# A gate's offset added by TensorE in the accumulation instead of by VectorE behind it

## The chip, the cores and the metric

The kernel runs on one core of a Trainium2 chip. The metric is the device time of one execution in microseconds (us). The engines are TensorE (PE, with its weight loads as PEld), VectorE (DVE), ScalarE (ACT), GpSimd (POOL) and SyncE (SP, which here only issues DMAs); PSUM is the memory that TensorE accumulates in, here eight banks of 128 partitions by 512 float32.

## The reference

One layer of an encoder for 2048 tokens of width 1024, in float32: a norm, a mixer, a second norm, and then a sum of three things that a third norm closes. The lines that matter here are these:

```
x = _layernorm(DEEPNORM_ALPHA * x + mix, ln1_g[i], ln1_b[i])
ffn = _hierarchical_moe(x, w_router_group[i], b_router_group[i], w_router_expert[i],
                        b_router_expert[i], w1[i], w3[i], w2[i])
ple = jax.nn.sigmoid(x @ w_ple_gate[i] + b_ple_gate[i]) * (p[i] @ w_ple_proj[i])
x = _layernorm(DEEPNORM_ALPHA * x + ffn + ple, ln2_g[i], ln2_b[i])
```

The experts (`ffn`) run for the two best of 32 experts for each token. The term `ple` is the embedding: a gate of 1024 by 1024 weights, with an offset `b_ple_gate` of 1024 numbers, times a product of 256 by 1024 weights.

## The kernel before

A tile is 128 tokens; there are 16. A float32 product is made of three fp32r matmuls (`mm3`, L221 to L224): each operand is split into a high and a low part, and high by high, high by low and low by high are accumulated in one PSUM bank. The splits are a cast on ScalarE (L356) and a subtraction on VectorE or GpSimd (L357).

The kernel goes through these stages: mixer, second norm and router; the embedding of tiles 10 and 11 and then 12 to 15 (`embed`, L1255), in among the last routing; the experts, as one long stretch of TensorE work; and the end, tiles 0 to 9, one `stage` each with a `last_stage` for tile 9 (from L1865). The end computes the embedding of its tile, adds the rows that the experts left in memory, and applies the third norm to that tile or to one of 10 to 15.

A gate of 512 columns is eight steps of three matmuls into one bank. With sigmoid(g) = (1 + tanh(g/2)) / 2 it then goes on like this:

- VectorE adds the offset, which stands in a buffer `RB[bp]` as 128 equal rows, and writes the sum to a buffer in `ZB`: L1280 in the embedding (12 times), L1862 in the end (19 times with 512 columns, twice with 256). This read frees the bank.
- ScalarE takes tanh in place in `ZB` (L1282, L1863).
- TensorE makes the product with `p`, two steps of three matmuls, in another bank (`embed_product`).
- VectorE multiplies (1 + tanh) by the product (L1286, L1889, L1925) and adds the result to the tile (L1290, L1892, L1926).

The last stage makes its products first and takes its gate in three parts, of 512, 256 and 256 columns; behind each part come multiplication, addition and statistics (L1928), and behind the third the norm in two halves with a write each (L1936).

In the end the inputs of a gate are transposed tiles that an earlier stage put in memory (`x1Td`), loaded by SyncE as a high and a low part into `FB`. The tile's own steps of the third norm are L1825 (adding an expert's row, twice), L1835 and L1837 on VectorE, L1836 (a square) on ScalarE, and L1849 with the write L1850, which ScalarE issues.

The order of the work is set in three ways. Generators are stepped in turn, one `yield` for some matmuls, and buffers are handed out from pools (`take`, `SR`, `SF`, `SP`, `SZ`), oldest first. A scheduler then places the instructions on each engine's queue by its own model of their times. In the end, VectorE's order is fixed as it is written (`pin`). Each engine runs its queue in order and waits on semaphores.

Of the kernel before, what the change touches and what calls it, by code (L numbers as in the profile page):

```python
# [17 lines left out]
D = 1024  # L18
KD = D // 128
# [164 lines left out]
def hybrid_conv_pool_hmoe_encoder(ctx, tc, x, p, ln0_g, ln0_b, w_in, b_in, conv_w, pool_w, pool_scale,  # L184
                                  w_o, ln1_g, ln1_b, w_rg, b_rg, w_re, b_re, w1, w3, w2, w_pg, b_pg,
                                  w_pp, ln2_g, ln2_b, out):
    nc = tc.nc
# [3 lines left out]
    FB, RB = Parts(), Parts()  # L191
# [29 lines left out]
    def mm3(o, ah, al, bh, bl, start, stop):  # L221
        nc.tensor.matmul(o, ah, bh, start=start, stop=False)  # L222
        nc.tensor.matmul(o, ah, bl, start=False, stop=False)  # L223
        nc.tensor.matmul(o, al, bh, start=False, stop=stop)  # L224

    def bcast(ap, n):
        return bass.AP(tensor=ap.tensor, offset=ap.offset, ap=[[0, 128], [1, n]])
# [28 lines left out]
    pidx = consts.tile([128, 1], F32, name="pidx")  # L256
# [70 lines left out]
    def need(name):  # L327

        if name in jobs:
            gen = jobs.pop(name)  # L330
            n = 0
            while next(gen, DONE) is not DONE:
                n += 1
                if n > 40:
                    bg.step()
            bg.forget(gen)
# [450 lines left out]
    v = RB[:, wrr, :KD * 36].rearrange("p (k e) -> p k e", e=36)  # L787
# [386 lines left out]
    def take(slots, m=1, align=1):  # L1174
        n = 0
        while not slots.has(m, align):
            bg.step()
            n += 1
            assert n < 10000, "no slot"
        return slots.get(m, align)  # L1180
# [74 lines left out]
    def lhs_tile(t, k):  # L1255
        return [FB[:, q, k * 128:(k + 1) * 128] for q in xs[t]]

    def embed(ts, lhs, w, done, halves=(0, 1)):

        for h in halves:  # L1260
            cols = slice(h * 512, (h + 1) * 512)
            bs = {}
            for i in range(0, len(ts), 2):
                bs[ts[i]] = take(SP, 2, 2)
                bs[ts[i + 1]] = bs[ts[i]] + 1
            for i in range(4):
                wh, wl = w(5 * h + i)
                for j in range(2):
                    k = 2 * i + j
                    for t in ts:  # L1270
                        mm3(PS[:, bs[t]], *lhs(t, k), FB[:, wh, j * 512:(j + 1) * 512],
                            FB[:, wl, j * 512:(j + 1) * 512], k == 0, k == KD - 1)
                        yield
                SF.free(wh)
                SF.free(wl)
            wh, wl = w(5 * h + 4)
            for t in ts:
                z = take(SZ)
                v = ZB[:, z, :512]
                nc.vector.tensor_add(v, PS[:, bs[t]], RB[:, bp, cols])  # L1280
                SP.free(bs[t])
                nc.scalar.activation(v, v, AF.Tanh, scale=0.5)  # L1282
                need(f"p{t}")
                b = take(SP)
                yield from embed_product(t, PS[:, b], wh, wl)
                nc.vector.scalar_tensor_tensor(v, v, 1.0, PS[:, b], op0=OP.add, op1=OP.mult)  # L1286
                SP.free(b)
                need(f"x{ts[0]}")
                a = RB[:, base[t], cols]
                nc.vector.scalar_tensor_tensor(a, a, ALPHA, v, op0=OP.mult, op1=OP.add)  # L1290
                SZ.free(z)
                if h:
                    release_p(t)
                    done(t)
            SF.free(wh)
            SF.free(wl)
# [37 lines left out]
    for ts in groups:  # L1334
# [9 lines left out]
        c, q = divmod(ts[-1], 4)  # L1344
# [18 lines left out]
    late = ctx.enter_context(tc.tile_pool(name="late", bufs=1))  # L1363
    RB.add(late.tile([128, NY, 1024], F32, name="RY", align_bytes=64), NR, NY)
    SR.add(NR, NY)
    bp = SR.get()
    nc.gpsimd.dma_start(RB[:, bp], bcast(b_pg, D))
    tz = SZ.get()
    prepare(PRE[0])
    w = weight("P", 0)  # L1370
# [90 lines left out]
    for r in ORDER:  # L1461
# [4 lines left out]
        for i in range(HALF[r]):  # L1466
            h = HCUM[r] + i
            f = FCUM[NE] + h // 2
            m = REST[r] if r in WIDE else 64
# [237 lines left out]
    with tc.For_i(0, nov_n, 1) as it:  # L1707
        z, zm = SZ.get(), SZ.get()
# [4 lines left out]
        b = SP.get()  # L1713
        for q in range(2 * NT):
            i, t = divmod(q, NT)
            v = ZB[:, z, (q % 4) * 128:(q % 4) * 128 + 128]
# [75 lines left out]
    def pin(ins):  # L1792

        if pinned:
            tc.add_manual_dep(ins.ins, pinned[-1].ins.name,
                              mybir.DependencyInfo(mybir.DependencyClass.NoSync, mybir.DependencyReason.DATA),
                              reason="in order")
        pinned.append(ins)
# [53 lines left out]

    def gates(t, parts):
        for b, h, lo, hi in parts:
            for k in range(KD):
                wh, wl = (FB[:, q, k % 2 * 512 + lo:k % 2 * 512 + hi] for q in ws[5 * h + k // 2])
                mm3(PS[:, b, :hi - lo], *lhs_tile(t, k), wh, wl, k == 0, k == KD - 1)
                yield

    def gate_end(z, o, cols):  # L1860
        v = ZB[:, z, :cols.stop - cols.start]
        pin(nc.vector.tensor_add(v, o, RB[:, bp, cols]))  # L1862
        nc.scalar.activation(v, v, AF.Tanh, scale=0.5)  # L1863
        return v

    def stage(i, t, ahead, behind):

        if i % 2 == 0 and 6 <= i + 4 < len(END):
            start_fetch(END[i + 4:i + 6])
        need(f"x{t}")  # L1870
        b = take(SP, 2, 2)
        yield from gates(t, [(b, 0, 0, 512), (b + 1, 1, 0, 512)])
        for q in xs.pop(t):
            SF.free(q)
        if i + 2 < len(END) and i % 2 == 0 and i + 2 >= 6:
            need(f"fetch{END[i + 2]}")
        prepare_tile(i + 2)
        zs = [take(SZ), take(SZ)]
        vs = [gate_end(zs[h], PS[:, b + h], slice(h * 512, (h + 1) * 512)) for h in range(2)]
        SP.free(b, 2)  # L1880
        for f in ahead:
            norm_begin(f)
        norm_end()
        need(f"p{t}")
        a = RB[:, base[t]]
        for h in range(2):
            m = take(SP)
            yield from embed_product(t, PS[:, m], *ws[5 * h + 4])
            pin(nc.vector.scalar_tensor_tensor(vs[h], vs[h], 1.0, PS[:, m], op0=OP.add, op1=OP.mult))  # L1889
            SP.free(m)  # L1890
            ah = a[:, h * 512:(h + 1) * 512]
            pin(nc.vector.scalar_tensor_tensor(ah, ah, ALPHA, vs[h], op0=OP.mult, op1=OP.add))  # L1892
            SZ.free(zs[h])
        release_p(t)
        for f in behind:
            norm_begin(f)
            if len(waiting) > 1:
                norm_end()

    def last_stage(t):  # L1900

        need(f"x{t}")
        until(lambda: t in arrived)
        a = RB[:, base[t]]
        need(f"p{t}")
        m = take(SP, 2, 2)
        for h in range(2):
            yield from embed_product(t, PS[:, m + h], *ws[5 * h + 4])
        release_p(t)
        pin(nc.vector.scalar_tensor_tensor(a, a, ALPHA, PS[:, m:m + 2].rearrange("p a c -> p (a c)"),  # L1910
                                           op0=OP.mult, op1=OP.add))
        add_rows(t)
        for i in range(2):
            SR.free(yq.pop((t, i)))
        st = stats[:, 4:6].rearrange("p a b -> p (a b)")
        for lo, hi in ((0, 512), (512, 768), (768, 1024)):
            h, cols, part = lo // 512, slice(lo, hi), slice(lo % 512, (hi - 1) % 512 + 1)
            b = take(SP)
            yield from gates(t, [(b, h, part.start, part.stop)])
            if h == 0:  # L1920
                norm_end()
            z = take(SZ)
            v = gate_end(z, PS[:, b, :hi - lo], cols)
            SP.free(b)
            pin(nc.vector.tensor_mul(v, v, PS[:, m + h, part]))  # L1925
            pin(nc.vector.tensor_add(a[:, cols], a[:, cols], v))  # L1926
            for q in range(lo // 256, hi // 256):
                pin(nc.vector.bn_stats(st[:, 6 * q:6 * q + 6], a[:, q * 256:(q + 1) * 256]))  # L1928
            SZ.free(z)
        nc.vector.bn_aggr(mv[:, 0], st)  # L1930
        nc.vector.tensor_scalar(rstd[:, 0:1], mv[:, 0, 1:2], EPS, None, op0=OP.add)
        nc.gpsimd.tensor_tensor(rstd[:, 0:1], rstd[:, 0:1], mhalf[:, 0:1], op=OP.pow)
        for h, eng in enumerate((nc.sync, nc.scalar)):
            cols = slice(h * 512, (h + 1) * 512)
            ln_apply(a[:, cols], 0, RB[:, g2, cols], RB[:, b2, cols])
            eng.dma_start(outf[t * 128:(t + 1) * 128, cols], a[:, cols])  # L1936
# [45 lines left out]
```

## Time and profile before

| | us |
|---|---|
| median of 3 runs | 1600.15 (1597.69 to 1601.34) |
| profiled execution | 1601.28 |
| its span | 1599.6 |
| PE busy | 1550.9 (97%) |
| DVE busy | 1169.0 (73%) |
| ACT busy | 761.2 (48%) |
| POOL busy | 446.4 (28%) |

The profile is of one execution, and its span is the time from the first instruction to the last event. Busy time of PE counts pipelined matmuls: a row of one lasts longer than the distance to the next start, so distances between starts tell how fast they follow. In a row of a timeline, the bracket at the end gives the idle time of the engine before the instruction and what ended it; x2 stands for two instructions in one row. The granted clock is given as a share of TensorE's full speed.

### The profile page before, as it was taken

Reading aid. Unit: us, or ns where it says so; the run is one execution under the profiler, and the core shown is the slowest. Engines: PE = TensorE matmul, PEld = TensorE weight load, DVE = VectorE, ACT = ScalarE, POOL = GpSimd, SP = SyncE. Lnnn points to the kernel's source line nnn. Section 1 sums busy time; section 2 is a strip of 40 time slices with the busy share of each in tenths; the row PEclk is TensorE's granted clock in tenths of the full one; section 3 lists DMA queues with packets and bytes.
Section 4 is the critical chain, followed back from the end, with each engine's and each line's share of the span. In section 5 each row is a group of like instructions: output and inputs, shape, how many; then the busy total and the mean of one; then the engine's idle time right before and its main releaser. Section 6 shows DMA issues by size and latency. Waiting matters only on the chain.

```text
span 1599.6 us, 22570 instructions
## 1 busy us (share of the span) xinstructions
PE 1550.9 (97%) x7837; PEld 1309.8 (82%) x7837; DVE 1169.0 (73%) x1534; ACT 761.2 (48%) x1005; POOL 446.4 (28%) x628
## 2 busy tenths in 40 slices
PE   8999999999999999989999999999999999999994
PEld 7888878887888887778988998888888888878784
DVE  8968574345666767758879878878888777776987
ACT  6332332113111215037878777777787766662221
POOL 3537763441232225110313111111111010005530
PEclk9999999999999999999999999999999999999997
DMA  7546269986385537459798998999999887998971
GB/s 232 196 144 205 67 199 311 342 300 185 112 271 198 171 116 260 132 205 368 282 364 312 406 373 312 370 350 356 356 353 331 312 328 262 388 328 308 363 232 68
DMA packets 205613, 430.64 MB, mean 269 GB/s; under 512 B 19128, under 2 KB 70888, under 8 KB 205496
## 3 DMA queue, kind: packets, MB, share of 16 engines
q1 hardware_dynamic: 161952, 292.06, 51.1%
q0 software_dynamic: 35024, 125.65, 21.5%
q10 hardware_dynamic: 8520, 11.45, 2.1%
q8 instruction: 63, 1.03, 0.3%
q14 instruction: 54, 0.44, 0.1%
HBM read 331.95 MB, written 97.16 MB: 268 GB/s over the span
## 4 chain that ended last, share of the span: by engine, by line
PE 52%; DVE 1%; DMA 1%; ACT 0%; issue 0%; DVEq 0%; ACTq 0%
PE PS L222 12%; PE PS L224 12%; PE PS L223 12%; PE PS L1574 10%; PE PS L363 2%; PE PS L1520 1%; PE PS L1521 1%; PE PS L1644 1%; DMA FB<-x1Td 1%; PE PS L1438 0%; DMA based<-RY 0%; DVE RB L1825 0%; DVE FB L357 0%; ACT FB L356 0%; ACT RY L1686 0%
## 5 line engine op out<-in xcount | busy, mean ns | idle before, releaser
L223 PE MATMUL PS<-FB 128*128 128x512 f32 (+1 forms) x1364 | 527.0, 386 | 6.2 <-DVE FB L357 5.5
L222 PE MATMUL PS<-FB 128*128 128x512 f32 (+1 forms) x1284 | 496.9, 390 | 6.1 <-DVE ZB L1280 2.4
L224 PE MATMUL PS<-FB 128*128 128x512 f32 (+1 forms) x1284 | 494.9, 386 | 2.4 <-DMA FB<-x1Td 2.0
L357 DVE TENSOR_TENSOR FB<-RY,FB 128x1024 fp32r<-128x1024 f32 x243 | 292.4, 1228 | 52.0 <-ACT FB L356 34.7
L223 PEld LDWEIGHTS PS<-FB 128*128 128x128 f32 x1364 | 258.3, 189 | 56.7 <-DVE FB L357 6.5
L222 PEld LDWEIGHTS PS<-FB 128*128 128x128 f32 x1284 | 242.7, 189 | 54.8 <-ACT FB L356 3.5
L224 PEld LDWEIGHTS PS<-FB 128*128 128x128 f32 x1284 | 242.8, 189 | 51.7 <-DMA FB<-x1Td 2.4
L356 ACT CAST FB<-RY 128x1024 fp32r<-128x1024 f32 x247 | 252.5, 1051 | 59.3 <-PE PS L223 20.7
L357 DVE TENSOR_TENSOR FB<-RB,FB 128x1024 fp32r<-128x1024 f32 x197 | 238.4, 1225 | 47.3 <-ACT FB L356 38.5
L356 ACT CAST FB<-RB 128x1024 fp32r<-128x1024 f32 x201 | 207.3, 1051 | 117.5 <-PE PS L223 51.8
L1574 PE MATMUL PS<-FB 128*128 128x296 f32 (+15 forms) x1280 | 174.6, 296 | 3.8 <-issue 3.1
L1574 PEld LDWEIGHTS PS<-FB 128*128 128x128 f32 x1280 | 170.6, 191 | 5.2 <-issue 3.3
L356 ACT CAST FB<-PS 128x1024 fp32r<-128x1024 f32 (+9 forms) x142 | 81.7, 591 | 139.1 <-PE PS L363 83.4
L357 DVE TENSOR_TENSOR FB<-PS,FB 128x1024 fp32r<-128x1024 f32 (+9 forms) x142 | 95.9, 688 | 62.3 <-ACT FB L356 61.8
L223 PE MATMUL PS<-FB,FY 128*128 128x512 f32 x264 | 104.1, 394 | 0.0
L1387 POOL DMA_INDIRECT RY<-x1d,TBI x22 | 45.5, 2070 | 174.2 <-DVE FB L357 132.7
L222 PE MATMUL PS<-FB,FY 128*128 128x512 f32 x216 | 85.7, 397 | 0.0
L224 PE MATMUL PS<-FB,FY 128*128 128x512 f32 x216 | 85.4, 395 | 0.0
L356 ACT CAST FY<-RB 128x1024 fp32r<-128x1024 f32 (+1 forms) x30 | 31.0, 1034 | 110.8 <-PE PS L223 59.7
L1387 POOL DMA_INDIRECT RB<-x1d,TBI x18 | 37.3, 2073 | 153.7 <-DVE FB L357 78.3
L1687 POOL DMA_DIRECT2D yd<-RY x25 | 14.3, 572 | 230.9 <-ACT RY L1686 229.6
L222 PE MATMUL PS<-FY,FB 128*128 128x512 f32 x180 | 71.6, 398 | 0.0
(293 smaller groups left out, 2062.3 us busy)
## 6 DMA issues: line engine op xcount, KB each, us to landing
RY<-in_w_dram SPq DMA_DIRECT2D x233, 512.0 KB, 8.5
RB<-in_w_dram SPq DMA_DIRECT2D x151, 512.0 KB, 9.0
yd<-RB POOLq DMA_DIRECT2D x67, 512.0 KB, 8.0
RB<-in_w_in_dram SPq DMA_DIRECT2D x32, 512.0 KB, 5.7
yd<-RY POOLq DMA_DIRECT2D x25, 512.0 KB, 7.3
RB<-in_x_dram SPq DMA_DIRECT2D x24, 512.0 KB, 4.6
x1Td<-FB POOLq DMA_DIRECT2D x20, 512.0 KB, 6.1
FB<-x1Td SPq DMA_DIRECT2D x20, 512.0 KB, 7.8
```

The lines of the kernel that those rows point to most:

```text
L222: nc.tensor.matmul(o, ah, bh, start=start, stop=False)
L223: nc.tensor.matmul(o, ah, bl, start=False, stop=False)
L224: nc.tensor.matmul(o, al, bh, start=False, stop=stop)
L356: nc.scalar.copy(hi, src)
L357: eng.tensor_sub(lo, src, hi)
L363: nc.tensor.transpose(v[:, k], src[:, k * 128:(k + 1) * 128], ident)
L1387: nc.gpsimd.indirect_dma_start(out=RB[0:half or 128, rows[n]], out_offset=None, in_=x1d, in_offset=bass.IndirectOffsetOnAxis(ap=idx, axis=0))
L1520: nc.tensor.matmul(o, xs[0][:, c], wh, start=start, stop=False)
L1521: nc.tensor.matmul(o, xs[0][:, c], wl, start=False, stop=stop)
L1574: nc.tensor.matmul(o, u, v, start=k == 0 and q == 0, stop=k == KD - 1 and q == 1)
L1644: nc.tensor.transpose(v[:, k], g[:, k * 128:(k + 1) * 128], ident[0:m, 0:m])
L1687: nc.gpsimd.dma_start(dst(n), RB[:, q])
```

## The change

TensorE adds the offset. The eight lines of set-up behind the former `bp` split the 1024 offsets into three rows of bf16 whose sum is the offset: three copies of the offset are loaded into three partitions, and two rounds of a cast on ScalarE and a masked subtraction on VectorE leave in partition 0 the first bf16 part, in 1 the second and in 2 the third. Each gate then begins with one bf16 matmul of three rows, ones by these parts (`offset`), which starts the accumulation, and the `mm3` behind it all accumulate. VectorE's addition is gone; ScalarE reads the bank for tanh, and its read frees the bank. The lines behind the set-up have other numbers in the new file: the third norm's L1825, L1835, L1836, L1837, L1849 become L1841, L1851, L1852, L1853, L1865, tanh in the end L1879, L1889 and L1892 become L1905 and L1908, L1910 L1926, and L1925, L1926, L1928 become L1941, L1942, L1944.

```
--- before.py
+++ after.py
@@ -1263,13 +1263,15 @@
             for i in range(0, len(ts), 2):
                 bs[ts[i]] = take(SP, 2, 2)
                 bs[ts[i + 1]] = bs[ts[i]] + 1
+            for t in ts:
+                offset(PS[:, bs[t]], h, 0, 512)
             for i in range(4):
                 wh, wl = w(5 * h + i)
                 for j in range(2):
                     k = 2 * i + j
                     for t in ts:
                         mm3(PS[:, bs[t]], *lhs(t, k), FB[:, wh, j * 512:(j + 1) * 512],
-                            FB[:, wl, j * 512:(j + 1) * 512], k == 0, k == KD - 1)
+                            FB[:, wl, j * 512:(j + 1) * 512], False, k == KD - 1)
                         yield
                 SF.free(wh)
                 SF.free(wl)
@@ -1277,9 +1279,8 @@
             for t in ts:
                 z = take(SZ)
                 v = ZB[:, z, :512]
-                nc.vector.tensor_add(v, PS[:, bs[t]], RB[:, bp, cols])
+                nc.scalar.activation(v, PS[:, bs[t]], AF.Tanh, scale=0.5)
                 SP.free(bs[t])
-                nc.scalar.activation(v, v, AF.Tanh, scale=0.5)
                 need(f"p{t}")
                 b = take(SP)
                 yield from embed_product(t, PS[:, b], wh, wl)
@@ -1363,8 +1364,23 @@
     late = ctx.enter_context(tc.tile_pool(name="late", bufs=1))
     RB.add(late.tile([128, NY, 1024], F32, name="RY", align_bytes=64), NR, NY)
     SR.add(NR, NY)
-    bp = SR.get()
-    nc.gpsimd.dma_start(RB[:, bp], bcast(b_pg, D))
+
+    bp, q = SR.get(), SR.get()
+    bpg, one = RB[0:3, bp, :512].bitcast(BF), RB[0:3, bp, 512:576].bitcast(BF)
+    v = RB[0:3, q]
+    nc.gpsimd.dma_start(v, bass.AP(tensor=b_pg.tensor, offset=b_pg.offset, ap=[[0, 3], [1, D]]))
+    nc.gpsimd.memset(one, 1.0)
+    for i in range(2):
+        m = RB[0:3, bp, 576 + i:577 + i]
+        nc.vector.tensor_scalar(m, pidx[0:3], float(i), None, op0=OP.is_gt)
+        nc.scalar.copy(bpg, v)
+        nc.vector.scalar_tensor_tensor(v, bpg, m, v, op0=OP.mult, op1=OP.subtract)
+    nc.scalar.copy(bpg, v)
+    SR.free(q)
+
+    def offset(o, h, lo, hi):
+        nc.tensor.matmul(o, one, bpg[:, h * 512 + lo:h * 512 + hi], start=True, stop=False)
+
     tz = SZ.get()
     prepare(PRE[0])
     w = weight("P", 0)
@@ -1852,15 +1868,15 @@
 
     def gates(t, parts):
         for b, h, lo, hi in parts:
+            offset(PS[:, b, :hi - lo], h, lo, hi)
             for k in range(KD):
                 wh, wl = (FB[:, q, k % 2 * 512 + lo:k % 2 * 512 + hi] for q in ws[5 * h + k // 2])
-                mm3(PS[:, b, :hi - lo], *lhs_tile(t, k), wh, wl, k == 0, k == KD - 1)
+                mm3(PS[:, b, :hi - lo], *lhs_tile(t, k), wh, wl, False, k == KD - 1)
                 yield
 
-    def gate_end(z, o, cols):
-        v = ZB[:, z, :cols.stop - cols.start]
-        pin(nc.vector.tensor_add(v, o, RB[:, bp, cols]))
-        nc.scalar.activation(v, v, AF.Tanh, scale=0.5)
+    def gate_end(z, o):
+        v = ZB[:, z, :o.shape[-1]]
+        nc.scalar.activation(v, o, AF.Tanh, scale=0.5)
         return v
 
     def stage(i, t, ahead, behind):
@@ -1876,7 +1892,7 @@
             need(f"fetch{END[i + 2]}")
         prepare_tile(i + 2)
         zs = [take(SZ), take(SZ)]
-        vs = [gate_end(zs[h], PS[:, b + h], slice(h * 512, (h + 1) * 512)) for h in range(2)]
+        vs = [gate_end(zs[h], PS[:, b + h]) for h in range(2)]
         SP.free(b, 2)
         for f in ahead:
             norm_begin(f)
@@ -1920,7 +1936,7 @@
             if h == 0:
                 norm_end()
             z = take(SZ)
-            v = gate_end(z, PS[:, b, :hi - lo], cols)
+            v = gate_end(z, PS[:, b, :hi - lo])
             SP.free(b)
             pin(nc.vector.tensor_mul(v, v, PS[:, m + h, part]))
             pin(nc.vector.tensor_add(a[:, cols], a[:, cols], v))
```

The scheduler places the embedding and the end anew. On TensorE, in the embedding, this is where a gate of tiles 12 to 15 begins (`PS` are banks, `FB` split operands, `RB` holds the offset's parts; a bracket names the engine or the DMA queue whose semaphore is waited for). Before:

```order
L224 MATMUL PS<-FB 128x512
L222 MATMUL PS<-FB 128x512
L223 MATMUL PS<-FB 128x512
L224 MATMUL PS<-FB 128x512
L222 MATMUL PS<-FB 128x512 [waits DVE_49]
L223 MATMUL PS<-FB 128x512
L224 MATMUL PS<-FB 128x512
```

And now:

```order
L224 MATMUL PS<-FB 128x512
L1221 MATMUL PS<-ident,RB 128x128 [waits DMAHW1_49]
L1221 MATMUL PS<-ident,RB 128x128 x3
L1382 LDWEIGHTS RB
L1382 MATMUL PS<-RB 128x512 [waits Activation_49]
L222 MATMUL PS<-FB 128x512
L223 MATMUL PS<-FB 128x512
```

The gate's first matmul waited for VectorE; now the offset's matmul is the first, and it waits for ScalarE. Four transposes of `p` (L1221) have come to stand ahead of it.

On TensorE in the end, this is where the gate of the sixth tile begins, whose transposed inputs come from memory. Before:

```order
L222 MATMUL PS<-FB 128x512 [waits DMAHW2_49,DVE_49]
L223 MATMUL PS<-FB 128x512
L222 MATMUL PS<-FB 128x512 [waits DVE_49]
L223 MATMUL PS<-FB 128x512
L224 MATMUL PS<-FB 128x512
L222 MATMUL PS<-FB 128x512
L223 MATMUL PS<-FB 128x512
L224 MATMUL PS<-FB 128x512
L224 MATMUL PS<-FB 128x512 [waits DMAHW2_49]
```

And now:

```order
L224 MATMUL PS<-FB 128x512
L1382 LDWEIGHTS RB
L1382 MATMUL PS<-RB 128x512 [waits DVE_49]
L222 MATMUL PS<-FB 128x512 [waits DMAHW7_49]
L223 MATMUL PS<-FB 128x512
L224 MATMUL PS<-FB 128x512 [waits DMAHW3_49]
```

Before, the gate's first two matmuls stood ahead of six others, and the first that needs the low part came behind them. Now the gate stands in one piece behind its offset, and each stage of the end has on TensorE an offset and a gate, an offset and a gate, and two products.

On VectorE, at the beginning of the last stage's sums. Before:

```order
L1849 SCALAR_TENSOR_TENSOR RB<-RB,rstd 128x1024
L1862 TENSOR_TENSOR ZB<-PS,RB 128x512
L1925 TENSOR_TENSOR ZB<-ZB,PS 128x512
L1926 TENSOR_TENSOR RB<-RB,ZB 128x512
L1928 BN_STATS stats<-RB 128x6 x2
L1862 TENSOR_TENSOR ZB<-PS,RB 128x256
```

And now:

```order
L1865 SCALAR_TENSOR_TENSOR RB<-RB,rstd 128x1024
L1941 TENSOR_TENSOR ZB<-ZB,PS 128x512
L1942 TENSOR_TENSOR RY<-RY,ZB 128x512
L1944 BN_STATS stats<-RY 128x6 x2
L1941 TENSOR_TENSOR ZB<-ZB,PS 128x256
```

The additions of the offset are gone from this queue, and the rest stands in the order that it had.

## Rows read from the trace of the kernel before

**Rows 1.** The stretches, core 0: length, busy time (count) by engine, PEclk, DMA share, GB/s

```profile
590.00:660.00 70.00, 64.24 (x302) 50.96 (x301) 50.16 (x91) 26.22 (x33) 25.10 (x15) 0.93 0.61 215
660.00:725.00 65.00, 59.75 (x299) 50.23 (x299) 43.77 (x76) 18.40 (x27) 8.96 (x10) 0.95 0.50 175
725.00:1440.00 715.00, 711.38 (x3888) 616.57 (x3887) 574.51 (x635) 522.62 (x668) 109.99 (x85) 1.00 0.92 343
1440.00:1580.00 140.00, 136.13 (x621) 113.00 (x619) 117.81 (x151) 32.11 (x52) 59.11 (x62) 0.99 0.75 269
1580.00:1600.00 20.00, 0.00 (x0) 0.00 (x0) 9.26 (x20) 1.46 (x3) 0.99 (x1) 0.53 0.13 52
```

**Rows 2.** Timeline of the end: start, duration, engine, line, operation, out<-in, idle before

```profile
1576.74 0.28 PE L224 MATMUL PS<-FB 128*128 128x256 f32 x1
...
1577.82 0.28 PE L224 MATMUL PS<-FB 128*128 128x256 f32 x1
...
1581.57 0.69 DVE L1925 TENSOR_TENSOR ZB<-ZB,PS 128x512 f32<-128x512 f32 x1 [0.69 <-ACT ZB L1863]
...
1585.84 0.41 DVE L1862 TENSOR_TENSOR ZB<-PS,RB 128x256 f32<-128x256 f32 x1
1586.28 0.42 ACT L1863 ACTIVATE ZB<-ZB 128x256 f32<-128x256 f32 x1 [1.73 <-DVE ZB L1862]
1586.72 0.42 DVE L1925 TENSOR_TENSOR ZB<-ZB,PS 128x256 f32<-128x256 f32 x1 [0.48 <-ACT ZB L1863]
```

**Rows 3.** Timeline of VectorE in the last stages

```profile
1557.43 0.69 DVE L1862 TENSOR_TENSOR ZB<-PS,RB 128x512 f32<-128x512 f32 x1 [3.39 <-PE PS L224]
...
1566.03 1.28 DVE L1862 TENSOR_TENSOR ZB<-PS,RB 128x512 f32<-128x512 f32 x2
```

**Rows 4.** Timeline of TensorE around its first stop

```profile
640.76 0.39 PE L224 MATMUL PS<-FB 128*128 128x512 f32 x1
...
643.48 0.39 PE L224 MATMUL PS<-FB 128*128 128x512 f32 x1
646.30 0.79 PE L222 MATMUL PS<-FB 128*128 128x512 f32 x1 [2.43 <-DVE ZB L1280]
...
649.44 0.39 PE L223 MATMUL PS<-FB 128*128 128x512 f32 x1
```

**Rows 5.** Timeline of VectorE and ScalarE at the same stop

```profile
645.56 0.68 DVE L1280 TENSOR_TENSOR ZB<-PS,RB 128x512 f32<-128x512 f32 x1
...
646.28 0.63 ACT L1282 ACTIVATE ZB<-ZB 128x512 f32<-128x512 f32 x1 [6.70 <-DVE ZB L1280]
```

**Rows 6.** Timeline of TensorE around its second stop

```profile
1509.56 0.39 PE L224 MATMUL PS<-FB 128*128 128x512 f32 x1
1511.92 0.50 PE L224 MATMUL PS<-FB 128*128 128x512 f32 x1 [1.97 <-DMA FB<-x1Td]
...
1516.59 0.39 PE L222 MATMUL PS<-FB 128*128 128x512 f32 x1
```

**Rows 7.** Timeline of TensorE, bf16 matmuls and what follows them

```profile
618.76 0.47 PE L1006 MATMUL PS<-OH,RB 128*128 128x32 bf16 x12
619.08 0.47 PE L222 MATMUL PS<-FB 128*128 128x512 f32 x1
619.39 0.39 PE L223 MATMUL PS<-FB 128*128 128x512 f32 x1
...
652.26 1.80 PE L1026 MATMUL PS<-OH,RB 128*128 128x480 bf16 x15
```

**Rows 8.** The page's groups, ScalarE's wide casts: busy, mean ns, idle before, releaser

```profile
L356 ACT CAST FB<-RB 128x1024 fp32r<-128x1024 f32 x201 | 207.3, 1051 | 117.5 <-PE PS L223 51.8
```

**Rows 9.** Waits from 600 to 722: total us, times, longest

```profile
ACT FB L356 <- DMA RB<-in_w_ple_gate_dram: 3.5, 1, 3.5
...
PE PS L223 <- DVE FB L357: 3.2, 1, 3.2
```

**Rows 10.** Groups by line and shape, the gates' addition in the end

```profile
L1862 DVE TENSOR_TENSOR ZB<-PS,RB 128x512 f32<-128x512 f32 x19 | 12.6, 685 | 21.4 <-PE PS L224 21.4
```

More of the change, by code (lines that the diff above doesn't have):

```diff
@@ L1265, in embed @@
                 bs[ts[i + 1]] = bs[ts[i]] + 1
+            for t in ts:
+                offset(PS[:, bs[t]], h, 0, 512)
             for i in range(4):
@@ L1271, in embed @@
                         mm3(PS[:, bs[t]], *lhs(t, k), FB[:, wh, j * 512:(j + 1) * 512],
-                            FB[:, wl, j * 512:(j + 1) * 512], k == 0, k == KD - 1)
+                            FB[:, wl, j * 512:(j + 1) * 512], False, k == KD - 1)
                         yield
@@ L1279, in embed @@
                 v = ZB[:, z, :512]
-                nc.vector.tensor_add(v, PS[:, bs[t]], RB[:, bp, cols])
+                nc.scalar.activation(v, PS[:, bs[t]], AF.Tanh, scale=0.5)
                 SP.free(bs[t])
-                nc.scalar.activation(v, v, AF.Tanh, scale=0.5)
                 need(f"p{t}")
@@ L1365, in hybrid_conv_pool_hmoe_encoder, with offset @@
     SR.add(NR, NY)
-    bp = SR.get()
-    nc.gpsimd.dma_start(RB[:, bp], bcast(b_pg, D))
+    bp, q = SR.get(), SR.get()
+    bpg, one = RB[0:3, bp, :512].bitcast(BF), RB[0:3, bp, 512:576].bitcast(BF)
+    v = RB[0:3, q]
+    nc.gpsimd.dma_start(v, bass.AP(tensor=b_pg.tensor, offset=b_pg.offset, ap=[[0, 3], [1, D]]))
+    nc.gpsimd.memset(one, 1.0)
+    for i in range(2):
+        m = RB[0:3, bp, 576 + i:577 + i]
+        nc.vector.tensor_scalar(m, pidx[0:3], float(i), None, op0=OP.is_gt)
+        nc.scalar.copy(bpg, v)
+        nc.vector.scalar_tensor_tensor(v, bpg, m, v, op0=OP.mult, op1=OP.subtract)
+    nc.scalar.copy(bpg, v)
+    SR.free(q)
+    def offset(o, h, lo, hi):
+        nc.tensor.matmul(o, one, bpg[:, h * 512 + lo:h * 512 + hi], start=True, stop=False)
     tz = SZ.get()
@@ L1854, in gates, with gate_end @@
         for b, h, lo, hi in parts:
+            offset(PS[:, b, :hi - lo], h, lo, hi)
             for k in range(KD):
                 wh, wl = (FB[:, q, k % 2 * 512 + lo:k % 2 * 512 + hi] for q in ws[5 * h + k // 2])
-                mm3(PS[:, b, :hi - lo], *lhs_tile(t, k), wh, wl, k == 0, k == KD - 1)
+                mm3(PS[:, b, :hi - lo], *lhs_tile(t, k), wh, wl, False, k == KD - 1)
                 yield
[L1860 to L1863, printed above, removed]
+    def gate_end(z, o):
+        v = ZB[:, z, :o.shape[-1]]
+        nc.scalar.activation(v, o, AF.Tanh, scale=0.5)
         return v
@@ L1878, in stage @@
         zs = [take(SZ), take(SZ)]
-        vs = [gate_end(zs[h], PS[:, b + h], slice(h * 512, (h + 1) * 512)) for h in range(2)]
+        vs = [gate_end(zs[h], PS[:, b + h]) for h in range(2)]
         SP.free(b, 2)
@@ L1922, in last_stage @@
             z = take(SZ)
-            v = gate_end(z, PS[:, b, :hi - lo], cols)
+            v = gate_end(z, PS[:, b, :hi - lo])
             SP.free(b)
```

## The prediction

> **What bounds the kernel now.** I read the busy time by stretch first. TensorE works 711 of the 715 us of the expert part, 64.2 of 70 and 59.8 of 65 us around the embedding, 136 of the 140 us before 1580, and none of the last 20, in which VectorE has 9.3 us [rows 1]. So the kernel is bound by TensorE up to its last matmul, and by VectorE and the last write behind it. The change adds TensorE work and takes VectorE work away; it can win only where TensorE stands still, and it touches only the two stages that hold gates: the embedding (about 598 to 720) and the end (1436 to 1600). The instructions of the other stretches keep their order.
>
> Second, the timeline behind TensorE's end. Its last matmul starts at 1577.82 and takes 0.28, so it ends at 1578.1; the third product of a gate, L1925, starts on VectorE at 1586.72 [rows 2]. VectorE is 8.6 us late there. It last waited for TensorE at 1557.43 (3.39 us) [rows 3]; from there it has work without a gap but for three waits for tanh, 0.69 and twice 0.48 [rows 2]. From the third L1925 to the end of the span are 1599.6 - 1586.72 = 12.9 us, which the change leaves alone.
>
> Third, TensorE's stops. At 643.48 it waits 2.43 us for L1280, VectorE's addition, which frees the PSUM bank [rows 4]. That addition started at 645.56, in a row of small instructions of the routing; ScalarE meanwhile stood idle for 6.7 us [rows 5]. At 1509.56 it waits 1.97 us for a transposed tile from memory [rows 6]. Behind the stop matmuls start every 0.45 us (646.30 to 649.44 are seven spacings) and not every 0.227 (640.76 to 643.48 are twelve) [rows 4]: the granted clock is at the lower of its two levels (1.2 GHz) for those 3 us, which shows in the 0.93 of the stretch [rows 1].
>
> **The change part by part.** All of it is set against the profiled execution itself, 1601.28 us (span 1599.6 and 1.7 outside it), which is 1.1 above the median of the runs.
>
> *The offsets on TensorE.* 12 in the embedding, 19 of 512 columns and 2 of 256 in the end. No row shows a matmul of three rows. Neighbours from both sides: a whole fp32r matmul of 512 columns, 0.227 [rows 4], and one of 256, 0.12 (1576.74 to 1577.82 are nine spacings) [rows 2]; the fifteen bf16 matmuls of L1026 have 3840 columns in 1.80 us, so 0.24 for 512 [rows 7]; a switch of type costs something too, since after twelve small bf16 matmuls the next fp32r one takes 0.31 and not 0.23 to its successor (619.08 to 619.39) [rows 7], so at most 0.31 each. Below, 0.2. I take 0.227, the nearest row: 12 x 0.227 = 2.7 in the embedding, 19 x 0.227 + 2 x 0.12 = 4.55 in the end, 7.3 together; ends 6.4 and 10.
>
> On whether three rows are cheap the Trainium skill, "TensorE: Matmul & The Clock Gate", section "LDWEIGHTS (loading the stationary operand)", says that a weight load's time hangs on its columns and not on the depth of the contraction. Here all 128 columns stay, so by it a three-row offset costs as much as a full step, as I price it; if the time went with the rows (3 of 128) the offsets would be nearly free and the sum 7 us lower. No run here shows a short contraction yet. The same page, section "Back-to-back issue gap", gives about 131 ns per 512-column matmul in a stream, by which the 33 would cost about 4.3 us; the 0.227 of this trace disagrees, and I keep the row.
>
> *The setup.* One load of 512 KB becomes one of 12 KB; ScalarE gets three casts of 1024 columns (1.05 each, by the same shape) [rows 8], VectorE two passes and two tiny ones, some 6 us in a chain. The first offset stands at about 598, and VectorE and ScalarE have gaps in that stretch. I take 0; if the chain came late it would cost the wait only, up to 3 or 4 with the slow clock behind it.
>
> *The embedding.* ScalarE takes the bank directly, and the offset that starts the next gate waits for ScalarE where it waited for VectorE. At the stop of 643.48 ScalarE was idle, so tanh runs as TensorE finishes, and the wait goes. From 643.48 to 649.44 there are 8 spacings in 5.96 us, which take 1.82 at full clock: 4.1 us to win [rows 4]. What waits there next are weights: the other stop of this stage, 3.2 us for L357 on VectorE, is a weight split [rows 9], which I leave where it is; VectorE has twelve additions of 0.68 less ahead of it, so it may shrink by about 1, which stays out of the sum. Term: 2.7 - 4.1 = -1.4.
>
> *The end: order.* Before, banks came back late, and TensorE did the gates of two tiles ahead of their products. Now each tile goes offset, gate, offset, gate, two products. A tile's loads then go out as the tile two places ahead is through, a whole stage (48 + 12 matmuls and two offsets, 14.1 us) before they are used. The stop for the load should go. From 1509.56 to 1516.59 are 14 spacings in 7.03 us; at full clock 3.18: 3.85 to win [rows 6].
>
> *The end: the tail.* VectorE loses 21 additions, 12.6 us for the wide ones [rows 10] and 0.8 for the two of 0.41. Does it keep up? From its first addition of the last tile but one (1566.03) to the third L1925 (1586.72) are 20.7 us [rows 2, 3]; less five additions (3 x 0.68 + 2 x 0.41 = 2.9) and the tanh waits (1.65) 16.2, plus about 0.9 for the first tanh: 17.1. TensorE has behind the same gate 24 product matmuls (5.45), 25 x 0.227 = 5.7 and 50 x 0.12 = 6.0: 17.1. A tie: VectorE is no longer behind by more than about 1. Then the third L1925 starts one tanh of 0.42 [rows 2] and some 0.2 of handing over behind TensorE's end: 0.6 and not 8.6, so -8.0.
>
> Sum: +2.7 - 4.1 + 4.55 - 3.85 - 8.0 = -8.7, so 1592.6; I say 1592.5. Without either stop's relief the sum is 7.3 - 8.0 = -0.7: the offsets eat what the tail gives, and all the gain hangs on the stops.
>
> **The rivals.**
> 1. *One stop stays.* For: the second stop is a matter of DMA, which are busy 0.75 of the time in that stretch [rows 1]; the first is one bank in a dense stretch, and behind it the next bank may be late. Then -4.6 to -4.9: 1596.5.
> 2. *Both stay or come back elsewhere.* For: TensorE had 5.8 and 5.3 us without work in the two stretches around the embedding [rows 1], and a stop that goes may only bring it sooner to a weight that isn't there. Against: ScalarE's idle 6.7 us. 1600.6, no change.
> 3. *Slower: tanh held up on ScalarE.* In the embedding ScalarE also casts the gate's weights, in order, and one of these casts waited 3.5 us for its load [rows 9]. A tanh behind such a cast keeps its bank, and the offset that wants the bank stops TensorE. Each such stop costs what the measured one cost with the slow clock behind it, 4.1. With both old stops still there it decides from the first: 1600.6 + 4.1 = 1604.7; with one of them gone, from the second. Offsets of 0.31 instead (+2.7) alone make 1603.3. Against: the routing's instructions on ScalarE are short, and it is free for most of the stretch (26 of 70 us busy) [rows 1].
> 4. *It doesn't do what it says.* ScalarE issues the writes of finished tiles, which wait for VectorE, and tanh stands in the same queue. If VectorE stays behind, only the last tile's own additions and waits leave the tail: 1.5 + 1.65 = 3.2 of the 8.0, and the sum with both stops gone is -3.9: 1597.4.
>
> **How the numbers follow.** Forecast (both stops go, tail short) 0.44, with a range of its own of 1589.5 to 1595.5; rival 1 0.23; rival 4 0.06; rival 2 0.13; rival 3 0.14. A measurement of this kernel tells about 0.2%, 3.2 us, from no change: faster is below 1597.0. Faster: 0.44 + 0.23 and nothing of rival 4, 0.67; same 0.06 + 0.13 = 0.19; slower 0.14. The range takes in the forecast with free offsets or an L357 wait that shrinks (1587), and goes up to rival 2 (1601.5); rival 3 is left out.
>
> **What would show it.** The offset: two starts on TensorE around L1382 0.23 apart. The embedding: no wait of a gate's first matmul for a bank; the stretch's matmul spacing at 0.227. The end: no wait for the transposed tiles; VectorE waiting for TensorE in each of the last stages; less than 1.5 us between TensorE's end and the third L1941. Wrong it would be with a new wait of L1382 for ScalarE, with the load wait back under another tile, or with VectorE at work for 5 us or more behind TensorE's end before that instruction.

## The result and the profile after

| | us | against before, 95% interval |
|---|---|---|
| before, median of 10 runs | 1601.0 | |
| changed, median of 10 runs | 1609.42 | 1.0053 (1.0043 to 1.0064) |
| changed, span of the profiled execution | 1608.5 | (before 1599.6) |

The changed kernel is slower by 8.4 us; I had forecast 1592.5, and the range ended at 1601.5. These are the stretches of the changed kernel, in the columns of [rows 1] (the five engines are PE, PEld, DVE, ACT and POOL, in this order):

```profile
590.00:660.00 70.00, 65.25 (x316) 50.31 (x315) 46.24 (x81) 25.59 (x32) 24.45 (x15) 0.98 0.61 215
660.00:725.00 65.00, 61.49 (x280) 49.27 (x278) 37.92 (x70) 13.71 (x23) 6.27 (x7) 0.89 0.41 146
725.00:1440.00 715.00, 710.06 (x3879) 616.81 (x3877) 572.20 (x632) 522.88 (x667) 120.07 (x87) 1.00 0.91 339
1440.00:1580.00 140.00, 138.08 (x595) 107.31 (x594) 102.51 (x127) 34.36 (x55) 61.95 (x61) 1.00 0.81 299
1580.00:1610.00 30.00, 15.27 (x88) 12.50 (x86) 17.97 (x28) 2.61 (x5) 1.73 (x3) 0.83 0.09 36
```

TensorE is busier and VectorE less busy in the end (102.5 and not 117.8 us up to 1580), as meant, and yet TensorE works 15 us into the last stretch. The second stretch shows a granted clock of 0.89 (0.95 before). Where the 8.9 us of the span come from shows in one mark, TensorE's first matmul behind the wait at the start of the expert loop. Before, then changed, each from TensorE's timeline:

```profile
720.67 14.67 PE L1574 MATMUL PS<-FB 128*128 128x384 f32 x90 [3.05 <-issue]
```

```profile
729.95 5.33 PE L1590 MATMUL PS<-FB 128*128 128x384 f32 x19 [3.17 <-issue]
```

The loop starts 9.3 us later; from there to the end of the span are 878.9 us before and 878.6 after. So the loss is there when the loop starts, most of it from the embedding, and the end, where the tail should have given 8 and a stop nearly 4, comes out even.

**The offset's price.** TensorE of the changed kernel, at an offset in the end; the matmul ahead of it is the last one of a product:

```profile
1505.22 0.39 PE L224 MATMUL PS<-FB 128*128 128x512 f32 x1
1505.54 0.39 PE L1382 MATMUL PS<-RB 3*128 3x512 bf16 x1
1505.86 0.50 PE L222 MATMUL PS<-FB 128*128 128x512 f32 x1
1506.19 0.40 PE L223 MATMUL PS<-FB 128*128 128x512 f32 x1
```

From L224 to L223 are 0.97 us where two usual spacings, without the offset between, are 0.455: the offset costs 0.515 and not 0.227. All three spacings around it are too long: 0.32 into it, 0.32 out of it, and 0.33 for the next. With 256 columns it is 0.41. That makes 31 x 0.515 + 2 x 0.41 = 16.8 us for 33 offsets, or 16.2 since two of them stand right behind another and cost 0.22 (below), against 7.3 in the forecast.

**The stop in the embedding.** The bank's wait of [rows 4] is gone, and this stands in its place; TensorE again:

```profile
642.78 0.39 PE L224 MATMUL PS<-FB 128*128 128x512 f32 x1
646.66 0.66 PE L1221 MATMUL PS<-ident,RB 128*128 128x128 f32 x4 [3.49 <-DMA RB<-in_p_dram]
647.25 0.39 PE L1382 MATMUL PS<-RB 3*128 3x512 bf16 x1
...
650.29 0.63 PE L222 MATMUL PS<-FB 128*128 128x512 f32 x1
```

The four transposes of `p`, which the scheduler (the planner in the texts of some runs) moved ahead of the offset, wait for their load, 3.49 us and the slow clock behind it (0.63 in a row is the long form of a matmul at the lower level). With it the stop costs 5.2 us against the same instructions at full clock, where the bank's stop cost 4.1.

**The routing's small matmuls.** Before, the 64 matmuls of 40 columns (L1094) stood in two runs of 32 with gate matmuls between; in the changed kernel they stand together. Before, then changed:

```profile
676.14 3.66 PE L1094 MATMUL PS<-RB,RY 128*128 128x40 f32 x32
...
685.44 3.66 PE L1094 MATMUL PS<-RB,RY 128*128 128x40 f32 x32
```

```profile
688.54 10.85 PE L1094 MATMUL PS<-RB,RY 128*128 128x40 f32 x64
699.88 0.58 PE L1382 MATMUL PS<-RB 3*128 3x512 bf16 x1 [0.49 <-DVE TBH L1100]
700.39 0.80 PE L222 MATMUL PS<-FB 128*128 128x512 f32 x1
```

Two runs of 3.66 have become one of 10.85. The granted clock is 0.99 from 688.5 to 692 and 0.50 from there to 699.4; over 688 to 706 it is 0.62:

```profile
688.00:706.00 18.00, 17.46 (x83) 15.49 (x82) 6.40 (x7) 2.67 (x4) 2.96 (x3) 0.62 0.56 202
```

**The tail.** TensorE's last matmul, the third tanh, and the third L1941 of the changed kernel answer to [rows 2]:

```profile
1594.99 0.28 PE L224 MATMUL PS<-FB 128*128 128x256 f32 x1
...
1595.31 0.38 ACT L1879 ACTIVATE ZB<-PS 128x256 f32<-128x256 f32 x1 [2.90 <-PE PS L224]
1595.72 0.42 DVE L1941 TENSOR_TENSOR ZB<-ZB,PS 128x256 f32<-128x256 f32 x1 [1.70 <-ACT ZB L1879]
```

TensorE ends at 1595.27, and the product starts 0.45 behind it, where it was 8.6. That step came as worked out. So did the stop of [rows 6]: TensorE no longer waits for a transposed tile.

### The profile page after: what moved, and what is told of

Read it like the earlier page. It is cut to its first block, busy times and chain, and to the rows that moved or that the text cites. A ratio compares the mean times of both kernels' runs of the same rounds, so it can differ in the third digit from the quotient of the medians.

```text
span 1608.5 us, 22606 instructions
## 1 busy us (share of the span) xinstructions
PE 1568.7 (98%) x7869; PEld 1315.0 (82%) x7870; DVE 1152.8 (72%) x1505; ACT 762.3 (47%) x1008; POOL 454.1 (28%) x629
## 4 chain that ended last, share of the span: by engine, by line
PE 53%; DVE 1%; issue 0%; ACT 0%; DMA 0%; DVEq 0%; ACTq 0%
PE PS L222 12%; PE PS L224 12%; PE PS L223 12%; PE PS L1590 10%; PE PS L363 2%; PE PS L1536 1%; PE PS L1537 1%; PE PS L1660 1%; PE PS L1382 0%; PE PS L1454 0%; DVE FB L357 0%; DMA based<-RB 0%; ACT FB L356 0%; PE PS L1221 0%; DVE FB L1148 0%
## 5 line engine op out<-in xcount | busy, mean ns | idle before, releaser
L223 PE MATMUL PS<-FB 128*128 128x512 f32 (+1 forms) x1364 | 527.2, 387 | 4.2 <-DVE FB L357 3.5
L224 PE MATMUL PS<-FB 128*128 128x512 f32 (+1 forms) x1284 | 495.2, 387 | 0.6 <-DVE FB L357 0.4
L223 PEld LDWEIGHTS PS<-FB 128*128 128x128 f32 x1364 | 258.4, 190 | 53.5 <-DVE FB L357 4.4
L224 PEld LDWEIGHTS PS<-FB 128*128 128x128 f32 x1284 | 243.0, 189 | 49.1 <-DVE FB L357 1.7
L1403 POOL DMA_INDIRECT RY<-x1d,TBI x23 | 55.5, 2413 | 184.4 <-DVE FB L357 97.0
L223 PE MATMUL PS<-FB,FY 128*128 128x512 f32 x264 | 104.2, 395 | 0.0
L224 PE MATMUL PS<-FB,FY 128*128 128x512 f32 x216 | 85.5, 396 | 0.0
L222 PE MATMUL PS<-FY,FB 128*128 128x512 f32 x180 | 71.6, 398 | 0.0
L224 PE MATMUL PS<-FY,FB 128*128 128x512 f32 x180 | 70.9, 395 | 0.0
```

Source lines behind the costliest of these rows:

```text
L1403: nc.gpsimd.indirect_dma_start(out=RB[0:half or 128, rows[n]], out_offset=None, in_=x1d, in_offset=bass.IndirectOffsetOnAxis(ap=idx, axis=0))
```

## The experiments

The medians of before lie between 1599.84 and 1601.18 in the runs beside them. "Loop" is the mark above (720.67 before), "rest" the time from it to the end of the span (878.9 before, 878.6 changed). Both are from one execution of each program, and single executions of before lie between 1596.22 and 1606.33, so 2 or 3 us between two marks can be chance.

| run | median us | ratio to before | loop | rest |
|---|---|---|---|---|
| fp32r_rows | 1624.72 | 1.0147 (1.0126 to 1.0168) | 745.08 | 880.3 |
| bf16_128_rows | 1601.56 | 1.0006 (0.9993 to 1.0018) | 727.41 | 870.9 |
| bf16_64_rows | 1611.29, one run | | 730.82 | 878.8 |
| end_only | 1595.27 | 0.9964 (0.9952 to 0.9976) | 716.73 | 875.4 |
| embedding_only | 1614.97 | 1.0084 (1.0066 to 1.0102) | 738.82 | 874.8 |
| end_only_128 | 1593.92 | 0.9959 (0.9947 to 0.9971) | 719.88 | 870.5 |
| late_p_128 | 1596.07 | 0.9973 (0.9962 to 0.9984) | 721.12 | 873.1 |
| last_stage_only | 1598.20 | 0.9995 (0.9986 to 1.0005) | 721.90 | 875.8 |
| routing_together | 1602.61 | 1.0018 (1.0006 to 1.0030) | 730.53 | 871.7 |

### What an offset's matmul costs

My theory from the rows was that the change of type, fp32r to bf16 and back, costs the time. The first run takes the type away (its buffers are fp32r tiles of their own, for which `RY` has a slot less):

```
-    bp, q = SR.get(), SR.get()
-    bpg, one = RB[0:3, bp, :512].bitcast(BF), RB[0:3, bp, 512:576].bitcast(BF)
+    q = SR.get()
+    bpg, one = late.tile([3, D], F32R, name="offs"), late.tile([3, 128], F32R, name="one")
...
-    nc.gpsimd.memset(one, 1.0)
+    nc.gpsimd.memset(v[:, :128], 1.0)
+    nc.scalar.copy(one, v[:, :128])
```

> The three rows of the offset and the ones are fp32r, like the matmuls beside them, instead of bf16; nothing else is meant to change. Theory 'change of type': the offset's own matmul costs one spacing, 0.21 to 0.23 us, and the other 0.29 us of the 0.52 that each takes in the changed kernel come from going to bf16 and back. Then the offset stands at 0.23 and 33 x 0.29 = 9.6 us go: about 1600 against the changed kernel's 1609. Rival 'short contraction': the three-row shape costs it, whatever the type: 0.52 stays, 1609. Rival 'order': the offsets are not what costs, the moved instructions are: 0.23 or not, the time stays within 3 us of 1609.

The theory fell. The offset in fp32r, with three rows, on TensorE:

```profile
1526.61 0.39 PE L225 MATMUL PS<-FB 128*128 128x512 f32 x1
1526.93 0.50 PE L1385 MATMUL PS<-offs,one 3*128 3x512 f32 x1
1527.35 0.50 PE L223 MATMUL PS<-FB 128*128 128x512 f32 x1
1527.69 0.40 PE L224 MATMUL PS<-FB 128*128 128x512 f32 x1
```

1.08 less 0.455 is 0.625: without a change of type the offset costs more, not less. (Nearly all of this run's 15 us above the changed kernel are lost in the embedding: its loop starts 15 us later than there, among others because the first offset waits 4.16 us for the set-up's last cast.)

The second run keeps bf16 and gives the matmul 128 rows; ones stand in three of them:

```
-    bpg, one = RB[0:3, bp, :512].bitcast(BF), RB[0:3, bp, 512:576].bitcast(BF)
-    v = RB[0:3, q]
+    bpg, one = RB[:, bp, :512].bitcast(BF), RB[:, bp, 512:576].bitcast(BF)
+    v = RB[:, q]
...
-    nc.gpsimd.memset(one, 1.0)
+    nc.gpsimd.memset(one, 0.0)
+    nc.gpsimd.memset(one[0:3], 1.0)
```

> The offset's matmul keeps bf16 but has 128 rows, three of ones and 125 of zeros, against 128 rows of parts. Theory 'change of type': 0.52 us each stays, 1609 within 2. Rival 'short contraction': a full contraction has none of the cost, 0.23 each and about 1600.

It came out as the rival "short contraction" said. Its timeline at the same place:

```profile
1498.54 0.39 PE L224 MATMUL PS<-FB 128*128 128x512 f32 x1
1498.77 0.39 PE L1383 MATMUL PS<-RB 128*128 128x512 bf16 x1
1498.81 0.58 PE L222 MATMUL PS<-FB 128*128 128x512 f32 x1
1499.22 0.39 PE L223 MATMUL PS<-FB 128*128 128x512 f32 x1
```

0.68 less 0.455 is 0.225, one usual spacing; between matmuls of 128 rows the change of type costs nothing. (Starts are uneven there, 0.04 and 0.41, but their sum is what the next matmul sees.) The whole kernel is 7.9 us faster than with three rows; 33 x 0.29 is 9.6. The same program with 64 rows ran once:

```
-    bpg, one = RB[:, bp, :512].bitcast(BF), RB[:, bp, 512:576].bitcast(BF)
+    bpg, one = RB[:64, bp, :512].bitcast(BF), RB[:64, bp, 512:576].bitcast(BF)
```

> One look: the offset's matmul with 64 rows. If any contraction shorter than its neighbours' costs, the offset takes about 0.5 as with three rows; if only a very short one does, 0.24.

```profile
1512.13 0.39 PE L224 MATMUL PS<-FB 128*128 128x512 f32 x1
1512.45 0.39 PE L1383 MATMUL PS<-RB 64*128 64x512 bf16 x1
1512.77 0.50 PE L222 MATMUL PS<-FB 128*128 128x512 f32 x1
1513.10 0.39 PE L223 MATMUL PS<-FB 128*128 128x512 f32 x1
```

0.97, as with three. So of the contractions tried (3, 64, 128) both that are shorter than their neighbours' cost a little over half a microsecond. What costs is the passage from a 128-row matmul to a shorter one and back, and not the matmul: in the changed kernel's first two offsets, which stand in a row, the second adds 0.22 only.

The rows of the weight loads show where the 0.29 above a usual spacing lie. The changed kernel, at the offset shown above, and the offset in fp32r:

```profile
1505.00 0.19 PEld L224 LDWEIGHTS PS<-FB 128*128 128x128 f32 x1
1505.54 0.09 PEld L1382 LDWEIGHTS <-RB 3*128 3x128 bf16 x1 [0.35 <-issue]
1505.86 0.19 PEld L222 LDWEIGHTS PS<-FB 128*128 128x128 f32 x1 [0.23 <-issue]
```

```profile
1526.92 0.18 PEld L1385 LDWEIGHTS PS<-offs,one 3*128 3x128 f32 x1 [0.35 <-DVE RY L1868]
```

In the stream a load starts a whole spacing ahead of its own matmul, as that of L224 does (1505.00 and 1505.22). The offset's load and the one behind it start together with their own matmuls (1505.54 and 1505.86), so neither runs beside the matmul in front. Their 0.09 and 0.19 make 0.28 of the 0.29; in fp32r 0.18 and 0.19 make 0.37 of the 0.40. With 256 columns the excess is 0.29 again, since the loads are the same. In bf16_128_rows the load behind the offset starts at 1498.77, with the offset's matmul and ahead of its own. That the unhidden loads are the cause is my reading of these rows; no run changes the loads alone.

### One stage at a time

Each of the next two runs takes one stage of the change, with three rows; the other has before's code and its 128 equal rows in a buffer `bb`:

```
+    bb = SR.get()
+    nc.gpsimd.dma_start(RB[:, bb], bcast(b_pg, D))
...
-                nc.scalar.activation(v, PS[:, bs[t]], AF.Tanh, scale=0.5)
+                nc.vector.tensor_add(v, PS[:, bs[t]], RB[:, bb, cols])
                 SP.free(bs[t])
+                nc.scalar.activation(v, v, AF.Tanh, scale=0.5)
```

> The embedding has VectorE's addition as before, the end has the offset on TensorE. If the accounts of the two stages are right, the loss of the embedding (9.3 us by the loop's start in the two traces) goes and the end is worth 21 x 0.5 = 10.6 less 8.0 of the tail less 3.9 of the stop: 1600 within 2, no change against before. Rival: the end is what costs, the new order there holds TensorE up: 1605 or more.

> The embedding has the offset on TensorE, the end VectorE's addition as before. By the same accounts the loop starts about 9 us late and the end is as before: 1610 within 2. If the end of the changed kernel costs most, 1603 or less.

The signs came as expected: the embedding loses, the end does not. Both times lie some 5 us from the expected ones, outside the 2 us that I had allowed. In end_only the rest is 875.4, 3.5 below before, and the embedding, with VectorE's additions as before, is 3.9 shorter than before: the weight stop of [rows 9] is 1.1 there and not 3.2, without slow matmuls behind it (about -4.6), the slow clock behind L1094 did not come (-1.7), and the bank's stop is longer, 3.46 and not 2.43 (+2.4 with the slow clock behind it). Why these three changed no run shows. With VectorE's additions this stage started the loop at 716.7, 719.9, 720.7 and 721.9 in four programs (end_only, end_only_128, before, last_stage_only), so I can't explain less than some 3 us there. The rest is 3 us shorter than the changed kernel's 878.6, and 1.8 of them have a place, two waits at the beginning of the end that end_only has not:

```profile
1446.44 0.59 PE L1382 MATMUL PS<-RB 3*128 3x512 bf16 x2 [1.10 <-ACT RY L1702]
...
1448.28 0.50 PE L222 MATMUL PS<-FB 128*128 128x512 f32 x1 [0.67 <-ACT FB L356]
```

They are no loss against before, though, which has two like them:

```profile
1428.00 0.66 PE L1221 MATMUL PS<-ident,RY 128*128 128x128 f32 x4 [0.67 <-ACT RY L1686]
...
1436.14 0.50 PE L222 MATMUL PS<-FB 128*128 128x512 f32 x1 [1.15 <-ACT FB L356]
```

In embedding_only the loop starts at 738.8, 8.9 behind the changed kernel's, above all through two waits at its first gates:

```profile
605.34 1.08 PE L1221 MATMUL PS<-ident,RY 128*128 128x128 f32 x4 [5.56 <-DVE RB L352]
607.62 1.01 PE L1384 MATMUL PS<-RB 3*128 3x512 bf16 x2 [1.19 <-ACT RB L1380]
```

The second is the wait for the set-up's chain that I had priced at nothing; the first is a wait of other transposes, which the scheduler put in front. Its rest, 874.8 with VectorE's additions in the end, is 4.1 below before. The stop for the transposed tile did not come; in its place TensorE waits twice for VectorE's addition, 3.5 us together, and VectorE is then less late at the end:

```profile
1595.54 0.28 PE L224 MATMUL PS<-FB 128*128 128x256 f32 x1
...
1600.70 0.42 DVE L1943 TENSOR_TENSOR ZB<-ZB,PS 128x256 f32<-128x256 f32 x1 [0.48 <-ACT ZB L1881]
```

4.9 us from TensorE's end to the third product, where it was 8.6 with the same code for the end. So before's 8.6 and its stop hang on how that program happened to fall in place, and of the end's gain less belongs to the change than I had counted. What does belong to it: all eight programs with the offset in the whole end (all but before, embedding_only and last_stage_only) have 0.45 there and none has that stop.

With 128 rows in the end only:

> The embedding as before, the end with the offset on TensorE, now as a bf16 matmul of 128 rows (three of ones). If the price lies in the short contraction (0.52 with three rows, 0.24 with 128), this saves 21 x 0.28 = 5.9 us against the same kernel with three rows (1595.3): 1589.4 within 2. If the gain of the 128 rows came from elsewhere in the program, 1595.

The edit is that of bf16_128_rows on end_only. The rest went from 875.4 to 870.5, 4.9 of the 5.9 expected, but the loop starts 3.2 later, in an embedding that the edit doesn't touch. So the whole time is 1593.9, 1.4 below end_only, and the expected 1589.4 was missed. The intervals of the two overlap. Both beat both kernels; this one is at 0.9959 of before, 15.5 us below the changed one.

### The tail

Only the last stage's three gates get the offset (128 rows); the other 30 keep VectorE's addition:

```
-        vs = [gate_end(zs[h], PS[:, b + h]) for h in range(2)]
+        vs = [gate_sum(zs[h], PS[:, b + h], slice(h * 512, (h + 1) * 512)) for h in range(2)]
```

> Only the last stage's three gates have the offset on TensorE (128 rows) and tanh from PSUM; the other 30 keep VectorE's addition. Theory 'whole chain': VectorE is 8.6 us late at the end because of the additions of all stages, so only the last stage's own three additions (1.5) and three waits for tanh (1.65) leave the tail, less 0.2 that TensorE gets longer: 1598 within 2. Rival 'the last three': those three additions, each with a tanh that waits for it, are all that makes the tail late: 1593 to 1594, as with the offset in the whole end.

1598.2: "the last three" (1593 to 1594) is out. It lies where "whole chain" put it, but at 0.9995 of before it can't be told from no change either. Its last matmul and its third product of a gate (L1950 there):

```profile
1579.45 0.28 PE L224 MATMUL PS<-FB 128*128 128x256 f32 x1
...
1584.67 0.40 DVE L1950 TENSOR_TENSOR ZB<-ZB,PS 128x256 f32<-128x256 f32 x1
```

4.9 us behind TensorE and not 0.45, so the last three additions are not all of it: VectorE's work in the stages ahead makes it late. How much the three are worth by themselves stays open, since embedding_only, which kept them, also ended 4.9 behind. Two stops of TensorE in the end (2.1 and 1.9 us) were still there.

### What the embedding lost

The transposes of `p` are asked for later (in the program of bf16_128_rows):

```
             fetch_p(ts)
-            for _ in range(6):
+            for _ in range(16):
                 yield
```

> All gates with the 128-row offset (1601.6 so far); the four transposes of p are asked for sixteen steps behind their load and not six, so that the planner puts them later on TensorE. In its order the routing's 64 small matmuls (L1094) also fall apart into groups with gates between them. Theory 'moved instructions': the wait for p (3.7 us and some 1.5 of slow clock behind it) and the slow clock behind and in the 64 small matmuls (about 4 more than before) go: 1592 to 1594. Rival: what stood there is late for another reason, and the next wait takes its place: 1599 or more.

The order changed as said there, L1094 in groups of 16, 16 and 32. The time, 1596.1, lies between the expected 1592 to 1594 and the rival's 1599: the loop starts 6.3 us earlier than in bf16_128_rows, at before's place, and the wait for `p` is gone; the rest grew by 2.2, whose cause I did not trace. The 64 small matmuls, and what now waits at the next offset:

```profile
676.62 1.88 PE L1094 MATMUL PS<-RB,RY 128*128 128x40 f32 x16
...
678.55 1.88 PE L1094 MATMUL PS<-RB,RY 128*128 128x40 f32 x16
...
683.70 3.66 PE L1094 MATMUL PS<-RB,RY 128*128 128x40 f32 x32
```

```profile
647.20 0.38 PE L1383 MATMUL PS<-RB 128*128 128x512 bf16 x1 [1.14 <-ACT ZB L1282]
```

The second fence is a stop as in rival 3 of the prediction: tanh on ScalarE holds the bank, and that costs 1.1 here. But tanh was not behind a cast: ScalarE had stood idle for 5.01 us and was released by VectorE (L972, a step of the routing). Both edits of this run act together, so a last one does the opposite of one of them alone, in the program of end_only_128: the four placements are made first, and then all 64 matmuls.

```
-                for t in range(NT // 2):
...
+        for i in (1, 0):
+            for h in (1, 0):
+                pl, place = pls[2 * i + h]
+                for t in range(NT // 2):
```

> As end_only_128 (1593.9; embedding as before), but the routing's four groups of 16 small matmuls each (L1094) stand in one run on TensorE, as they do in the changed kernel. Theory: in one run of 64 the granted clock falls inside the run, and the second half takes twice the time: 11 us and not 7 for the 64, and slow matmuls behind them, 3.5 to 5.5 in all: 1597.5 to 1599.5. Rival: they cost the same wherever they stand, and the embedding lost its time elsewhere: 1594 within 1.5.

```profile
687.99 7.02 PE L1099 MATMUL PS<-RY 128*128 128x40 f32 x32 [2.77 <-issue]
694.81 7.03 PE L1099 MATMUL PS<-RB,RY 128*128 128x40 f32 x32
```

Each half takes 7.0 us and not 3.66, and the kernel is 8.7 us slower than end_only_128, outside the 3.5 to 5.5 that I expected: the first half was slow as well, behind a wait of 2.77 that the new order also brought. That wait and the run of 64 are not told apart here. Where no such wait stood in front, the clock fell inside the run: in the changed kernel (0.99, then 0.50), and in bf16_128_rows, where the first 32 took 3.66 and the other 32, 0.17 us behind them, 6.83. How much of the 8.7 is the clock's is not shown.

## Why the prediction was wrong

**The offsets on TensorE.** This step failed first. I took 0.227 and "at most 0.31 each"; they cost 0.515 (0.41 with 256 columns), 16.2 us and not 7.3. The upper bound rested on rows of a change of type [rows 7], and I counted a loss on one side of the offset only. The type was the wrong suspect: with 128 rows bf16 costs a usual spacing. I wrote that no run shows a short contraction yet; that was wrong. The price was to be read in the trace of before, at a bf16 matmul of 32 rows among the gate's:

```profile
658.29 0.39 PE L223 MATMUL PS<-FB 128*128 128x512 f32 x1
658.61 0.24 PE L1023 MATMUL PS<-ZB,RB 32*128 32x160 bf16 x1
658.78 0.50 PE L224 MATMUL PS<-FB 128*128 128x512 f32 x1
659.12 0.40 PE L222 MATMUL PS<-FB 128*128 128x512 f32 x1
```

It has the same 0.32 into it and 0.34 behind the next. 0.83 less 0.455 is 0.375 for 160 columns, where the bf16 rows of [rows 7] give 0.07, so 0.3 more, as with the offset. The nearest row to a three-row matmul was this one, not a whole fp32r matmul.

**The rules that I weighed.** The Trainium skill's "TensorE: Matmul & The Clock Gate", section "LDWEIGHTS (loading the stationary operand)", says that a weight load's time goes with its columns; the loads took 0.09 us with three rows and 0.10 with 128 (in fp32r 0.18 and 0.19), so the trace agrees, and three rows were not cheap. The section "Why this matters for your kernels" has a single matmul of K=32 take the same time as one of K=128. The rows' durations agree (0.39 with 3, 64 and 128 rows); their spacing in a stream of 128-row matmuls does not, 0.515 against 0.225, and the spacing is what the kernel pays.

**The embedding.** I forecast -1.4, and it was +9.3. The twelve offsets took 5.9 and not 2.7. The bank's stop went, as said, but the transposes of `p` waited in its place, 5.2 us for the 4.1 that I had counted as won: I had shown that they had come to stand ahead of the offset and had not asked when their load lands. The 64 small matmuls came together: 10.85 and 0.49 of a wait for 7.3, and some 0.8 more of slow clock behind them, about 5 us that stood in no term. One offset waited 0.83 for VectorE (L1037). Against it the weight stop of [rows 9], 3.2 us and slow matmuls, shrank to 1.2 and none, 4.6 us. That this came from VectorE's relief is not shown: the stop is 1.1 in end_only, which keeps the additions in the embedding, and 2.7 in bf16_128_rows, which has none. Set against before, these make +8.2. Another 1.5 was lost ahead of the first offset: the matmul in front of it starts at 599.32, and its like in before at 597.82. In bf16_64_rows, with the change as well, that is 598.01, so these 1.5 may be chance. Together that is 9.7, where 9.3 were measured.

**The end.** The terms were 4.55 - 3.85 - 8.0, a gain of 7.3. TensorE's end comes 8.3 us nearer to the end of the span, as worked out; the 0.2 of handing over in that term stood on no row, and it was 0.04 into tanh and 0.03 out of it. The stop went, 3.85, though not by this change alone. The offsets took 10.3. And the expert loop itself, from its mark to the first instruction of the end, was 1.4 us longer (707.45 and not 706.06), which I did not trace. So 0.4 was left of 7.3, and the term that was wrong is again the offsets.

**The tie** between VectorE and TensorE in the last stages was read rightly: VectorE waits for tanh 1.70 us before the third product and is 0.45 late. Rival 4 didn't come; rival 3 has its sign, but not its mechanism.

## What to carry to other kernels

A matmul whose contraction is shorter than its neighbours' costs time on both sides: pad its operands with zeros to their rows (0.29 us saved for each here), or put several in a row. Before an addition is moved to the bound engine, look at its price in a row of the same shape among the same neighbours, and at every instruction that the scheduler moves along with it: in the embedding the two groups that it moved cost some 10 us, where the change's own relief was to give 4.1. And a change with two places is worth trying one place at a time: one half of this one gains 0.4%, the other loses more.

## What the runs showed of the hardware

- bf16 and fp32r matmuls of 128 rows and 512 columns follow each other without loss (0.225 for a bf16 matmul between fp32r ones); 3 or 64 rows among 128 cost 0.515, in fp32r with 3 rows 0.625.
- The excess, 0.29 and 0.40, is about the sum of two weight loads, the short matmul's (0.09 in bf16, 0.18 in fp32r) and that of the matmul behind it (0.19), which start there together with their own matmuls.
- A second short matmul right behind the first adds 0.22 only.
- 32 matmuls of 40 columns in a row take 3.66 us at full clock; 64 in a row fell to the lower clock within the run (10.85; 3.66 and then 6.83), and once stood at it from the start (7.0 for each 32, behind a wait of 2.77).
